# Right sides of half-size products made in 16 steps beside seven plain pairs, and the opening squares on ScalarE

## The chip, the cores and the metric

The kernel runs on one core of a Trainium2 chip. Its time is the device time of one execution in microseconds (us). The kernel before took 2112.32 us (median of three runs, 2112.1 to 2113.64).

A core has five engines, each with its own queue that is worked off in order: TensorE (PE, matmuls; its weight loads are shown as PEld), VectorE (DVE), ScalarE (ACT), GpSimd (POOL) and SyncE (SP, which here issues the DMAs). Matmuls write into PSUM, which has eight banks of 128 x 512 float32.

## The reference, cut to what matters

A decoder trunk of two layers on a sequence of 512 tokens with 1024 channels, all in float32. Each layer has two feed-forwards, so there are four in the kernel; the change touches these alone.

```python
def rms_norm(x, g):
    xf = x.astype(F32)
    y = xf * lax.rsqrt(jnp.mean(xf * xf, axis=-1, keepdims=True) + EPS)
    return (y * g.astype(F32)).astype(x.dtype)

def swiglu_ffn(h, w_in, w_out):          # w_in: 1024 x 5632, w_out: 2816 x 1024
    g, u = jnp.split(h @ w_in, 2, axis=-1)
    return (jax.nn.silu(g) * u) @ w_out
...
    for i in range(DEPTH):               # DEPTH = 2
        x = x + 0.5 * swiglu_ffn(rms_norm(x, ffn1_norm[i]), ffn1_w_in[i], ffn1_w_out[i])
        ...                              # token mixer, cross-attention
        x = x + 0.5 * swiglu_ffn(rms_norm(x, ffn2_norm[i]), ffn2_w_in[i], ffn2_w_out[i])
```

## The kernel before

**Layout and precision.** Activations are held transposed: `x` is eight tiles of 128 channels x 512 tokens. Each float32 operand is split into a high part, a rounded copy made by ScalarE, and a low part, the difference, made by VectorE. A product is three matmuls: high by high, high by low, low by high (`mm3`, lines 395 to 397; the third needs the low part of the weights). The names in the profile: `whl` is a weight tile split in this way (ScalarE's copy at line 326, VectorE's subtraction at line 366), `wraw` the tile as the DMA brought it, `xg` the activations times the norm's gains, split, `hT` the hidden activations, split (lines 407 and 408 are the split of anything but weights).

**The weight stream.** All weights are packed in the order of their use, in tiles of 128 x 512. Four buffers hold raw tiles, seven hold split ones, and the split is issued five tiles ahead of use. A raw tile is fetched when an earlier one's buffer is free.

**A feed-forward** has 22 pairs of output blocks (128 columns of `g` and the 128 of `u`). It runs in this order (`ffn_steps`):

- `first`: pairs 0 and 1 at once, into four banks (`psf`), so that TensorE can start as soon as the first channels are there. On the way `norm_row` forms the norm's factor 1/rms as a row `rbc` spread over all partitions: a matmul with ones (`psn`, line 547), a square root on ScalarE (line 550) and a reciprocal on VectorE (line 551).
- plain pairs up to `NCL`: 48 matmuls of 512 columns each into two banks, `psg` and `psu`. Then `act` multiplies both with `rbc` (lines 601 and 603), takes SiLU on ScalarE (602), and `hidden` multiplies and splits them into `hT` (594, 407, 408).
- the other pairs by seven half-size products each (`seven`): the activations are cut into quarters, and seven sums of weight quarters (the left sides) meet seven sums of activation quarters (the right sides, `rhs`) in 84 matmuls of 256 columns into `psr`. The left sides are sums formed on VectorE (`wsum`, lines 351 to 359). The right sides need the norm applied; `right` forms them once in each feed-forward, for four `j` of 256 channels each: two scalings of `x` (line 616), four subtractions of 256 columns (619 to 622) and the split (407, 408).
- the out-projection (`psy`) in phases: each phase multiplies the hidden blocks that are there (`PHASES`), and `SLOTS` says how many of its eight outputs stand inside each set of seven products.

In the later three feed-forwards `right` is called behind `first`, before any plain pair; in the opening one, where the norm isn't known yet, after the first plain pair. The squares for the norm are made at the end of the stage before, by `squared` (a square on ScalarE, a sum on VectorE); in the opening they are made by GpSimd (line 675) and summed on VectorE (line 677).

**What sets the order.** A scheduler puts the instructions of each engine in a row when the program is built, from the order in which they are written, their dependencies and the free buffers. An engine then takes its row in order; an instruction that waits holds up all behind it. The `tmp` pool has five buffers, for `g`, `u`, squares and the four parts of a `j`.

Of the kernel before, what the change touches and what calls it, by code (L numbers as in the profile page):

```python
# [6 lines left out]
F32 = mybir.dt.float32  # L7
# [6 lines left out]
P = 128  # L14
D = 1024
S = 512
# [3 lines left out]
FK = DFF // P  # L20
# [31 lines left out]
NORMS = (3, 6, 3, 7)  # L52
# [19 lines left out]
def segs_dense(outs, k0=0, k1=DK):  # L72
    for name, c0 in outs:
        for k in range(k0, k1):
            yield (name, k * P, c0, P)


def cols(name, c0, n):
    return [(name, c0 + m * P) for m in range(n)]


def ffn_outs(f, l):
    return [(f"{f}_w_in/{l}", gu * DFF + i * P) for i in range(FK) for gu in range(2)]
# [1 line left out]

PHASES = ((0, 6), (6, 12), (12, 16), (16, FK))
NCL = PHASES[0][1]
SLOTS = (2, 1, 1, 2, 1, 1, 2, 2, 2, 2, 1, 1, 1, 1, 1, 1)  # L90


def ffn_steps():

    yield ("first",)
    for i in range(2, NCL):
        yield ("plain", i)
    outs = iter([("out", p, m) for p in range(len(PHASES) - 1) for m in range(DK)])
    for n in range(NCL, FK):
        for b in (1, 2, 5):  # L100
            yield ("seven", b, n)
        if n > NCL:
            yield ("seven", 4, n - 1)
            yield ("seven", 3, n - 1)
        yield ("seven", 6, n)
        for _ in range(SLOTS[n - NCL]):
            yield next(outs)
        yield ("seven", 7, n)
    yield next(outs)
    yield ("seven", 4, FK - 1)  # L110
    yield ("seven", 3, FK - 1)
    yield from outs
    for m in range(DK):
        yield ("out", len(PHASES) - 1, m)


def segs_ffn(f, l):
    outs, wo = ffn_outs(f, l), cols(f"{f}_w_out/{l}", 0, DK)
    for st in ffn_steps():
# [4 lines left out]
        elif st[0] == "out":  # L124
            if (f, l) == ("ffn2", DEPTH - 1) and st[1:] == (len(PHASES) - 1, DK - 1):
                yield None
            yield from segs_dense([wo[st[2]]], *PHASES[st[1]])
        else:
# [259 lines left out]
class Kernel:  # L388
# [194 lines left out]
    def ffn(self, f, l, gnext, opening=False, mid=(), final=False):  # L583
        nc, ws = self.nc, self.ws
# [4 lines left out]
        with pool(name="ht", bufs=12, reuse_waits="tile") as htp, pool(name="rhs", bufs=DK // 2) as rhsp:  # L589
# [9 lines left out]
            def act(psg, psu):  # L599
                g, u = self.tmp("g"), self.tmp("u")  # L600
                nc.vector.tensor_mul(g, psg, self.rbc)
                nc.scalar.activation(g, g, AF.Silu)
                nc.vector.tensor_mul(u, psu, self.rbc)
                hidden(g, u)

            rhs = []

            def right():


                for j in range(DK // 2):
                    t = rhsp.tile([P, 2, 7, H], F32R, name="rhs")
                    parts = [self.tmp(f"b{i}").rearrange("p (a n) -> p a n", a=2) for i in range(4)]
                    (b11, b12), (b21, b22), (t1, t3), (t2, t4) = ((q[:, 0], q[:, 1]) for q in parts)
                    for h in range(2):
                        nc.vector.scalar_tensor_tensor(parts[h].rearrange("p a n -> p (a n)"), self.x[2 * j + h],
                                                       self.vec(f"{f}_norm/{l}", 2 * j + h), self.rbc,
                                                       op0=ALU.mult, op1=ALU.mult)
                    nc.vector.tensor_sub(t1, b12, b11)
                    nc.vector.tensor_sub(t3, b22, b12)  # L620
                    nc.vector.tensor_sub(t2, b22, t1)
                    nc.vector.tensor_sub(t4, b21, t2)
                    self.split([t[:, p, 0] for p in range(2)], b11)
                    for i in range(3):
                        self.split([t[:, p, 1 + 2 * i:3 + 2 * i] for p in range(2)], parts[1 + i])
                    rhs.append(t)


            SIDES = {1: (0, 0), 2: (1, 1), 3: (2, 2), 4: (6, 0), 5: (3, 2), 6: (5, 0), 7: (4, 0)}
# [31 lines left out]
            outs = ffn_outs(f, l)  # L661
            wo = cols(f"{f}_w_out/{l}", 0, DK)
            last = len(PHASES) - 1
            for st in ffn_steps():
                if st[0] == "first":
                    pss = [self.bank("psf") for _ in range(4)]
                    if opening:
                        for k in range(2):
                            self.gained(k, f"{f}_norm/{l}")
                            ws.split(k + 1)  # L670
                        hooks = {k: lambda k=k: self.gained(k + 2, f"{f}_norm/{l}") for k in range(DK - 2)}
                        self.first(pss, outs[:4], self.xg, hooks=hooks)
                        for k in range(DK):
                            sq = self.tmp("sq") if k else self.bc.tile([P, S], F32, name="sqsum")
                            nc.gpsimd.tensor_mul(sq, self.x[k], self.x[k])
                            if k:
                                nc.vector.tensor_add(self.sqsum, self.sqsum, sq)
                            else:
                                self.sqsum = sq
                    else:  # L680
                        self.first(pss, outs[:4], self.xg, hooks={NORMS[0]: self.norm_row})
                        act(*pss[:2])
                        act(*pss[2:])
                        right()
                elif st[0] == "plain":
                    i = st[1]
                    psg, psu = self.bank("psg"), self.bank("psu")
                    self.dense(psg, outs[2 * i], self.xg)
                    if opening and i == 2:
                        self.norm_row()  # L690
                    self.dense(psu, outs[2 * i + 1], self.xg)
                    if opening and i == 2:
                        act(*pss[:2])
                        act(*pss[2:])
                    act(psg, psu)
                    if opening and i == 2:
                        right()
                elif st[0] == "seven":
                    seven(*st[1:])
                else:  # L700
                    ph, m = st[1:]
                    if final and ph == last:
                        with pool(name="kept", bufs=KEPT) as ws.kept_pool:
                            self.finish(wo, hT, *PHASES[last])
                        return
                    if (ph, m) == (1, 0):
                        next(mid, None)
                    ps = self.bank("psy")
                    self.dense(ps, wo[m], hT, *PHASES[ph])
                    nc.vector.scalar_tensor_tensor(self.x[m], ps, 0.5, self.x[m], op0=ALU.mult, op1=ALU.add)  # L710
                    if ph == last:
                        self.stage_x(m, gnext)
                    elif ph == 1:
                        next(mid, None)
# [825 lines left out]
```

## Time and profile before

| | |
|---|---|
| median of the runs | 2112.32 us |
| profiled execution, its own time | 2111.65 us |
| its span, first to last instruction | 2109.8 us |
| busy: TensorE, VectorE, ScalarE, GpSimd | 98%, 74%, 54%, 9% |
| mean granted TensorE clock | 0.988 of full |
| moved by DMA | 200.91 MB, 95 GB/s in the mean |

Times in the rows are us from the span's start unless marked ns. A row of a timeline gives start, duration, engine, line, instruction, output and inputs, shapes and count, and in brackets how long the engine stood idle before it and what ended that. Durations of one engine's instructions overlap at their ends, so the step from one start to the next is shorter than the duration. The granted clock is given as a share of 2.4 GHz.

### The profile page before, as it was taken

The page shows a single profiled execution, that of the slowest core. Times are in us where ns is not written, and L with a number is a line of the kernel's source. Part 1 is how long each engine was busy: PE and PEld are TensorE (multiplying, and loading weights), DVE is VectorE, ACT ScalarE, POOL GpSimd, SP SyncE. Part 2 cuts the span into 40 slices and gives each one's busy share as a digit, 9 for nine tenths or more (in the row PEclk, how much of TensorE's full clock was granted, in tenths as well). Part 3 has the DMA queues.
Part 4 walks back from the last instruction along what each step waited for, and adds up shares of the span by engine and source line. Part 5 has one row for each costly group of instructions (what it writes and reads, how often), then busy time and mean ns, then how long its engine had stood idle before and what let it go on. Part 6 is the DMA issues. An engine that isn't in the chain of part 4 may idle for free.

```text
span 2109.8 us, 33571 instructions
## 1 busy us (share of the span) xinstructions
PE 2058.1 (98%) x12400; PEld 1836.9 (87%) x12400; DVE 1562.5 (74%) x2834; ACT 1129.9 (54%) x2273; POOL 198.1 (9%) x269
## 2 busy tenths in 40 slices
PE   9799999999989999989999999999999998999997
PEld 6699998988879999878999988788998887899996
DVE  7877876865777777687777767788976557777774
ACT  5455555654535545554545545787775544455453
POOL 2000000000000000000000023444452100000000
PEclk9999999999999999999999999999999999999999
DMA  4333323432233332324332233311124222433222
GB/s 151 100 121 110 105 81 100 146 110 57 74 120 121 101 95 81 98 62 135 120 106 86 73 97 114 98 37 36 66 70 134 76 75 67 133 111 105 91 71 74
DMA packets 112212, 200.91 MB, mean 95 GB/s; under 512 B 12592, under 2 KB 19504, under 8 KB 112048
## 3 DMA queue, kind: packets, MB, share of 16 engines
q1 hardware_dynamic: 111360, 198.20, 30.4%
q8 instruction: 97, 1.59, 0.3%
q10 hardware_dynamic: 688, 0.58, 0.1%
q14 instruction: 67, 0.55, 0.1%
HBM read 196.63 MB, written 2.10 MB: 94 GB/s over the span
## 4 chain that ended last, share of the span: by engine, by line
PE 89%; DVE 7%; ACT 1%; issue 1%; DMA 1%; SPq 0%; DVEq 0%; ACTq 0%
PE psr L397 10%; PE psr L396 10%; PE psr L395 10%; PE psy L396 10%; PE psy L395 10%; PE psy L397 10%; PE pso L1358 2%; PE psq L397 2%; PE psq L396 2%; PE psq L395 2%; DVE rhs L408 2%; PE pst L1346 1%; PE psv L395 1%; PE psv L396 1%; PE psv L397 1%
## 5 line engine op out<-in xcount | busy, mean ns | idle before, releaser
L366 DVE TENSOR_TENSOR whl<-wraw,whl 128x512 fp32r<-128x512 f32 (+2 forms) x631 | 435.4, 693 | 227.4 <-ACT whl L326 213.1
L326 ACT CAST whl<-wraw 128x512 fp32r<-128x512 f32 (+3 forms) x685 | 415.4, 611 | 347.1 <-PE psy L397 92.0
L397 PE MATMUL psr<-rhs,whl 128*128 128x256 f32 x1792 | 506.9, 283 | 1.0 <-DVE whl L366 1.0
L395 PE MATMUL psr<-rhs,whl 128*128 128x256 f32 x1792 | 507.5, 283 | 0.2
L396 PE MATMUL psr<-rhs,whl 128*128 128x256 f32 x1792 | 507.1, 283 | 0.0
L395 PEld LDWEIGHTS psr<-rhs,whl 128*128 128x128 f32 x1792 | 343.5, 192 | 4.3 <-ACT whl L326 1.4
L396 PEld LDWEIGHTS psr<-rhs,whl 128*128 128x128 f32 x1792 | 343.5, 192 | 2.8
L397 PEld LDWEIGHTS psr<-rhs,whl 128*128 128x128 f32 x1792 | 343.2, 192 | 2.0 <-DVE whl L366 1.8
L396 PE MATMUL psy<-hT,whl 128*128 128x512 f32 (+1 forms) x710 | 276.2, 389 | 0.0
L395 PE MATMUL psy<-hT,whl 128*128 128x512 f32 (+1 forms) x710 | 275.9, 389 | 0.0
L397 PE MATMUL psy<-hT,whl 128*128 128x512 f32 (+1 forms) x710 | 275.1, 388 | 0.0
L326 ACT CAST whl<-wsum 128x512 fp32r<-128x512 f32 x256 | 159.3, 622 | 203.7 <-PE psy L397 155.6
L366 DVE TENSOR_TENSOR whl<-wsum,whl 128x512 fp32r<-128x512 f32 x256 | 176.1, 689 | 56.1 <-ACT whl L326 53.9
L397 PEld LDWEIGHTS psy<-hT,whl 128*128 128x128 f32 x710 | 133.4, 188 | 27.6
L396 PEld LDWEIGHTS psy<-hT,whl 128*128 128x128 f32 x710 | 133.6, 188 | 25.7 <-DVE hT L408 1.2
L395 PEld LDWEIGHTS psy<-hT,whl 128*128 128x128 f32 x710 | 133.6, 188 | 25.4
L366 POOL TENSOR_TENSOR whl<-wraw,whl 128x512 fp32r<-128x512 f32 (+2 forms) x54 | 70.0, 1298 | 846.2 <-ACT whl L326 840.8
L710 DVE SCALAR_TENSOR_TENSOR x<-psy,x 128x512 f32<-128x512 f32 x120 | 82.6, 689 | 43.3 <-PE psy L397 42.5
L1339 POOL TENSOR_SCALAR pr<-pr,smn,gates 128x128 f32<-128x128 f32 (+3 forms) x128 | 87.7, 696 | 98.7 <-DVE smn L1337 70.0
L397 PE MATMUL psu<-xg,whl 128*128 128x512 f32 x128 | 54.0, 422 | 29.1 <-DVE whl L366 29.1
L1330 ACT ACTIVATE pr<-pr,mxn 128x128 f32<-128x128 f32 (+3 forms) x128 | 71.3, 559 | 17.0 <-DVE mxn L1326 15.8
L395 PE MATMUL psq<-xg,whl 128*128 128x512 f32 x192 | 75.8, 395 | 0.0
(308 smaller groups left out, 3957.1 us busy)
## 6 DMA issues: line engine op xcount, KB each, us to landing
wraw<-wts SPq DMA_DIRECT2D x711, 256.0 KB, 2.8
wraw<-wts SPq DMA_DIRECT2D x18, 128.0 KB, 2.5
wraw<-wts SPq DMA_DIRECT2D x12, 192.0 KB, 2.5
x<-xT SPq DMA_DIRECT2D x8, 256.0 KB, 5.3
mraw<-memT SPq DMA_DIRECT2D x4, 512.0 KB, 3.6
out<-y SPq DMA_DIRECT2D x6, 256.0 KB, 2.6
wraw<-wts SPq DMA_DIRECT2D x8, 152.0 KB, 2.2
out<-y ACTq DMA_DIRECT2D x2, 256.0 KB, 2.9
```

Of the source, the lines that this page charges most:

```text
L326: nc.scalar.copy(self.hl[q][:, 0, :w], src[:, :w])
L366: eng.tensor_sub(hl[:, 1, :w], src[:, :w], hl[:, 0, :w].bitcast(F32))
L395: mm(ps, a[0], b[0], start=start, stop=False, **kw)
L396: mm(ps, a[0], b[1], start=False, stop=False, **kw)
L397: mm(ps, a[1], b[0], start=False, stop=stop, **kw)
L408: self.nc.vector.tensor_sub(hl[1], src, hl[0].bitcast(F32))
L710: nc.vector.scalar_tensor_tensor(self.x[m], ps, 0.5, self.x[m], op0=ALU.mult, op1=ALU.add)
L1330: nc.scalar.activation(pr[br][:, :nk], pr[br][:, :nk], AF.Exp, bias=mx[:, br:br + 1], scale=-1.0, accum_out=sums[:, br:br + 1])
L1339: nc.gpsimd.tensor_scalar(pr[br][:, :nk], pr[br][:, :nk], sums[:, br:br + 1], gt[:, i, h * 3 + 1 + br:h * 3 + 2 + br], op0=ALU.mult, op1=A ...
L1346: nc.tensor.transpose(pt[:, j * P:(j + 1) * P], pr[br][:, j * P:(j + 1) * P], self.identf)
L1358: nc.tensor.matmul(ps[:, c0:c0 + 256], v[br][j][:, g, :], pT[br][:, hl, j, :], start=False, stop=br == 1 and j == 2 * i2 + 1 and hl == 1)
```

## The change

The seven-product stage starts one pair later (`PHASES` begins with 7 in place of 6, and the second phase of the out-projection has 5 blocks in place of 6; `SLOTS` is fitted to it). `right` becomes a generator `rights` with four stops for each `j`, 16 in all. In the later three feed-forwards its first two steps are taken inside `first`, at channels 6 and 7; the rest are taken in the plain pairs, one for every five of the matmul groups that `dense_steps` counts, seven to a bank. What isn't done by the end of the last plain pair follows behind it. In the opening the steps begin in the second bank of the first plain pair, so that 12 of them stand beside pairs. The opening squares are made by `squared`, on ScalarE.

```diff
-PHASES = ((0, 6), (6, 12), (12, 16), (16, FK))
+PHASES = ((0, 7), (7, 12), (12, 16), (16, FK))
 NCL = PHASES[0][1]
-SLOTS = (2, 1, 1, 2, 1, 1, 2, 2, 2, 2, 1, 1, 1, 1, 1, 1)
+SLOTS = (2, 2, 2, 1, 1, 2, 2, 2, 2, 1, 1, 1, 1, 1, 1)
...
-            def right():
+            def rights():
...
                                                        op0=ALU.mult, op1=ALU.mult)
+                    yield
                     nc.vector.tensor_sub(t1, b12, b11)
                     nc.vector.tensor_sub(t3, b22, b12)
                     nc.vector.tensor_sub(t2, b22, t1)
                     nc.vector.tensor_sub(t4, b21, t2)
+                    yield
                     self.split([t[:, p, 0] for p in range(2)], b11)
                     for i in range(3):
                         self.split([t[:, p, 1 + 2 * i:3 + 2 * i] for p in range(2)], parts[1 + i])
+                        if i != 1:
+                            yield
                     rhs.append(t)
+
+            right = rights()
+
+            def plain(ps, out):
+
+                nonlocal count
+                for _ in self.dense_steps(ps, out, self.xg):
+                    count += 1
+                    if count % 5 == 0:
+                        next(right, None)
+
+            count = 0
...
                         for k in range(DK):
-                            sq = self.tmp("sq") if k else self.bc.tile([P, S], F32, name="sqsum")
-                            nc.gpsimd.tensor_mul(sq, self.x[k], self.x[k])
-                            if k:
-                                nc.vector.tensor_add(self.sqsum, self.sqsum, sq)
-                            else:
-                                self.sqsum = sq
+                            self.squared(k)
                     else:
-                        self.first(pss, outs[:4], self.xg, hooks={NORMS[0]: self.norm_row})
+                        self.first(pss, outs[:4], self.xg, hooks={NORMS[0]: self.norm_row, 6: lambda: next(right),
+                                                                 7: lambda: next(right)})
                         act(*pss[:2])
                         act(*pss[2:])
-                        right()
                 elif st[0] == "plain":
                     i = st[1]
                     psg, psu = self.bank("psg"), self.bank("psu")
-                    self.dense(psg, outs[2 * i], self.xg)
                     if opening and i == 2:
+                        self.dense(psg, outs[2 * i], self.xg)
                         self.norm_row()
-                    self.dense(psu, outs[2 * i + 1], self.xg)
+                    else:
+                        plain(psg, outs[2 * i])
+                    plain(psu, outs[2 * i + 1])
...
-                    if opening and i == 2:
-                        right()
+                    if i == NCL - 1:
+                        for _ in right:
+                            pass
```

Lines of the changed kernel behind the generator stand some 14 to 16 further down; `right`'s subtractions are lines 620 to 623 there.

**VectorE, second feed-forward (ffn2 of layer 0).** Before, the end of the block of right sides (`b` are the parts of a `j`) and the first low halves of weights (`whl`) behind it:

```order
L408 TENSOR_TENSOR rhs<-b_5775,rhs 128x256
L622 TENSOR_TENSOR b_5778<-b_5776,b_5778 128x256
L408 TENSOR_TENSOR rhs<-b_5776,rhs 128x512
L408 TENSOR_TENSOR rhs<-b_5777,rhs 128x512
L408 TENSOR_TENSOR rhs<-b_5778,rhs 128x512
L366 TENSOR_TENSOR whl<-wraw,whl 128x512 x2
L601 TENSOR_TENSOR g<-psg,rbc 128x512
```

Now, in the second plain pair of the same feed-forward:

```order
L366 TENSOR_TENSOR whl<-wraw,whl 128x512
L623 TENSOR_TENSOR b_5784<-b_5782,b_5784 128x256
L408 TENSOR_TENSOR rhs<-b_5781,rhs 128x256
L408 TENSOR_TENSOR rhs<-b_5782,rhs 128x512
L366 TENSOR_TENSOR whl<-wraw,whl 128x512
L601 TENSOR_TENSOR g<-psg,rbc 128x512
L366 TENSOR_TENSOR whl<-wraw,whl 128x512
L408 TENSOR_TENSOR rhs<-b_5783,rhs 128x512
L408 TENSOR_TENSOR rhs<-b_5784,rhs 128x512
L366 TENSOR_TENSOR whl<-wraw,whl 128x512
```

The low halves of weights now stand between the steps of a `j`, where before all four `j` stood in one piece with none among them.

**VectorE, opening feed-forward, behind the last plain pair.** Before, from the sum for the third product to the low halves behind the last read of `psu`:

```order
L353 TENSOR_TENSOR wsum<-wsum,wraw_661 128x512
L366 TENSOR_TENSOR whl<-wraw_664,whl 128x512
L366 TENSOR_TENSOR whl<-wsum,whl 128x512 x2
L603 TENSOR_TENSOR u<-psu,rbc 128x512
L366 TENSOR_TENSOR whl<-wraw,whl 128x512
L594 TENSOR_TENSOR u<-u,g 128x512
```

Now, from that read on:

```order
L603 TENSOR_TENSOR u<-psu,rbc 128x512
L616 SCALAR_TENSOR_TENSOR b_827<-x_109,vecsb,rbc 128x512
L594 TENSOR_TENSOR u<-u,g 128x512
L616 SCALAR_TENSOR_TENSOR b_828<-x_110,vecsb,rbc 128x512
L620 TENSOR_TENSOR b_829<-b_827 128x256
L408 TENSOR_TENSOR hT<-u,hT 128x512
L621 TENSOR_TENSOR b_829<-b_828,b_827 128x256
L622 TENSOR_TENSOR b_830<-b_828,b_829 128x256
L408 TENSOR_TENSOR rhs<-b_827,rhs 128x256
L623 TENSOR_TENSOR b_830<-b_828,b_830 128x256
L408 TENSOR_TENSOR rhs<-b_828,rhs 128x512
L408 TENSOR_TENSOR rhs<-b_829,rhs 128x512
```

The fourth `j` (of `x` 6 and 7) now stands here, behind the read of the last pair's second bank. Ahead of that read stand the same rows as before.

**TensorE at the same place**, now, with buffer numbers (`rhs_826` is the right side of the fourth `j`, the three `psr` belong to the first three products):

```order
L397 MATMUL psr_885<-rhs_698,whl_759 128x256
L395 MATMUL psy_927<-hT_438,whl_800 128x512
L396 MATMUL psy_927<-hT_438,whl_800 128x512
L395 MATMUL psy_956<-hT_438,whl_846 128x512
L396 MATMUL psy_956<-hT_438,whl_846 128x512
L395 MATMUL psr_845<-rhs_826,whl_708 128x256
L395 MATMUL psr_866<-rhs_826,whl_740 128x256
L395 MATMUL psr_885<-rhs_826,whl_759 128x256
L396 MATMUL psr_845<-rhs_826,whl_708 128x256
L397 MATMUL psr_845<-rhs_826,whl_708 128x256
```

Before, the first product ran through all four `j` before the second began; now the first three products take their first three `j`, and four out-projection matmuls are drawn forward, before the fourth.

## Rows read from the trace of the kernel before

**Rows 1.** Page, parts 1 and 4: busy share of TensorE; last chain by engine
```profile
PE 2058.1 (98%) x12400; PEld 1836.9 (87%) x12400; DVE 1562.5 (74%) x2834; ACT 1129.9 (54%) x2273; POOL 198.1 (9%) x269
...
PE 89%; DVE 7%; ACT 1%; issue 1%; DMA 1%; SPq 0%; DVEq 0%; ACTq 0%
```

**Rows 2.** Waits of TensorE over the whole span: us in total, times, longest
```profile
PE psu L397 <- DVE whl L366: 29.1, 4, 10.6
PE psf L397 <- DVE whl L366: 2.8, 2, 2.3
```

**Rows 3.** Timeline of VectorE, second feed-forward: start, us, instruction, idle before and its releaser
```profile
561.80 0.69 DVE L366 TENSOR_TENSOR whl<-wraw,whl 128x512 fp32r<-128x512 f32 x1 [2.03 <-ACT whl L326]
...
572.02 1.41 DVE L616 SCALAR_TENSOR_TENSOR b<-x,vecsb,rbc 128x512 f32<-128x512 f32 x2
573.34 0.42 DVE L619 TENSOR_TENSOR b<-b 128x256 f32<-128x256 f32 x1
573.68 0.42 DVE L620 TENSOR_TENSOR b<-b,b 128x256 f32<-128x256 f32 x1
...
576.83 1.41 DVE L616 SCALAR_TENSOR_TENSOR b<-x,vecsb,rbc 128x512 f32<-128x512 f32 x2
...
586.44 1.29 DVE L366 TENSOR_TENSOR whl<-wraw,whl 128x512 fp32r<-128x512 f32 x2
587.65 0.69 DVE L601 TENSOR_TENSOR g<-psg,rbc 128x512 f32<-128x512 f32 x1
```

**Rows 4.** Timeline of TensorE, second feed-forward, where it starts again
```profile
587.19 0.79 PE L397 MATMUL psu<-xg,whl 128*128 128x512 f32 x1 [6.18 <-DVE whl L366]
...
593.24 0.39 PE L397 MATMUL psu<-xg,whl 128*128 128x512 f32 x1
...
599.82 0.39 PE L395 MATMUL psu<-xg,whl 128*128 128x512 f32 x1
```

**Rows 5.** Timeline of TensorE, the same feed-forward, first half-size product
```profile
616.13 0.28 PE L395 MATMUL psr<-rhs,whl 128*128 128x256 f32 x1
...
617.45 0.28 PE L397 MATMUL psr<-rhs,whl 128*128 128x256 f32 x1
```

**Rows 6.** Busy by stretch: us, PE, PEld, DVE, ACT, POOL (x), clock, DMA, GB/s
```profile
70.40:73.90 3.50, 3.40 (x8) 2.73 (x9) 3.50 (x7) 1.59 (x3) 0.00 (x0) 0.51 0.41 152
587.10:592.70 5.60, 5.51 (x13) 4.35 (x14) 5.60 (x11) 2.29 (x4) 0.00 (x0) 0.51 0.51 165
944.60:947.60 3.00, 2.96 (x7) 2.38 (x8) 3.00 (x6) 1.14 (x2) 0.00 (x0) 0.50 0.45 166
1784.50:1790.60 6.10, 6.00 (x14) 4.75 (x15) 4.46 (x9) 2.09 (x4) 0.00 (x0) 0.50 0.58 175
17.00:22.00 5.00, 2.69 (x12) 1.91 (x11) 5.00 (x8) 0.62 (x1) 1.48 (x1) 1.00 0.12 15
625.00:700.00 75.00, 75.00 (x521) 70.31 (x521) 60.62 (x102) 37.00 (x73) 0.00 (x0) 1.00 0.39 122
```

**Rows 7.** Timeline of GpSimd, opening
```profile
7.81 5.58 POOL L675 TENSOR_TENSOR sq<-x 128x512 f32<-128x512 f32 x4 [0.87 <-DMA x<-xT]
```

**Rows 8.** Timeline of VectorE, opening and start of its half-size products
```profile
10.96 1.52 DVE L366 TENSOR_TENSOR whl<-wraw,whl 128x512 fp32r<-128x512 f32 x1
...
86.14 0.69 DVE L366 TENSOR_TENSOR whl<-wraw,whl 128x512 fp32r<-128x512 f32 x1 [3.09 <-ACT whl L326]
...
91.40 0.69 DVE L603 TENSOR_TENSOR u<-psu,rbc 128x512 f32<-128x512 f32 x1
```

**Rows 9.** Timeline of ScalarE, opening
```profile
4.46 0.72 ACT L492 ACTIVATE xg<-x,vecsb 128x512 fp32r<-128x512 f32 x1 [1.74 <-DMA x<-xT]
```

**Rows 10.** Timeline of TensorE, opening, start of its half-size products
```profile
87.60 0.28 PE L395 MATMUL psr<-rhs,whl 128*128 128x256 f32 x1
...
94.28 0.40 PE L395 MATMUL psy<-hT,whl 128*128 128x512 f32 x1
```

**Rows 11.** Timeline of ScalarE, a square of the later stages
```profile
542.93 0.62 ACT L505 ACTIVATE sq<-x 128x512 f32<-128x512 f32 x1
```

## The prediction

> **What bounds the kernel now.** I read the page first: TensorE is busy for 98% of the span, and the chain that ended last runs through it for 89% and through VectorE for 7% [rows 1]. So VectorE holds TensorE up somewhere, and the next view, TensorE's waits, says where: 29.1 us in four waits, the longest 10.6, all `psu` matmuls waiting for the low half of a weight tile (`whl`, line 366) [rows 2]. There are four feed-forwards, and each has one such wait.
>
> The third view is VectorE's timeline at one of them, the second (ffn2 of layer 0) [rows 3]. The low half at 561.80 is the last for a long time. Then VectorE multiplies out the heads of the first four banks and after that makes all right sides in one block: one `j` begins at 572.02, the next at 576.83, so a `j` takes 4.81 us and the four 19.2. The next low half stands at 586.44, 24.6 us after the last. TensorE starts again at 587.19 after 6.18 us of waiting [rows 4], so it ran dry at 581.0. It had lived on tiles split ahead for 18.6 us from the end of the last low half (about 562.4). Those 18.6 us are the lead with which I reckon below.
>
> Fourth, the stretches with their granted clock [rows 6]: after each of the four waits TensorE goes on at a clock of 0.50 to 0.51, which is the 1.2 GHz level. At 2.4 GHz a 512-wide matmul takes 0.227 us (29 steps from 593.24 to 599.82 [rows 4]) and a 256-wide one 0.120 (11 steps from 616.13 to 617.45 [rows 5]). In the stage of the half-size products TensorE is busy for 75.00 us of 75.00 and VectorE for 60.62 [rows 6]: nothing but the number of matmuls counts there.
>
> **The change, part by part.** I reckon against the profiled execution: span 2109.8, its own time 2111.65; the median of the runs is 2112.32, 0.67 more.
>
> (a) The block of right sides leaves VectorE's queue in front of the low halves. Its instructions stay the same: per `j` two scalings, four 256-wide subtractions, one 256-wide and three 512-wide low halves. Only their place changes: 14 of the 16 steps stand beside the plain pairs, two inside the first four banks. By the order of the second feed-forward there is now never more than about 4.5 us of other work between two low halves of plain tiles (four low halves of right sides, one of them 256 wide, and four reads of `psf`: 0.34 + 7 x 0.60 [rows 3]; 0.60 is half of 586.44 to 587.65, 0.34 is 573.34 to 573.68). Does VectorE's total fit? A plain pair takes TensorE 48 x 0.227 = 10.9 us. It costs VectorE four low halves and four instructions of `act`, 8 x 0.60 = 4.8, and now 19.2 / 5 = 3.84 of right sides: 8.6 of 10.9 us. With 18.6 us of lead at the start and less work than time, TensorE should not run dry in the last three feed-forwards, and the first wait of the opening goes as well. Gone: 29.1 us, and 4 x 0.16 = 0.6, since a wait is counted from a modelled end 0.39 after the matmul's start where the next would have started after 0.23. Bounds: none of it gone if the low halves were late again (rival 3), 29.7 at most.
>
> (b) With the waits go the falls of the clock. The four stretches at half clock are 3.50, 5.60, 3.00 and 6.10 us with 8, 13, 7 and 14 matmuls [rows 6]; at 0.227 each these would take 1.8, 3.0, 1.6 and 3.2. That is 8.6 us lost to the clock.
>
> (c) A seventh plain pair replaces one set of seven products in each feed-forward. Seven products are 84 matmuls of 256 columns, 84 x 0.120 = 10.1 us; a pair is 48 of 512, 10.9. TensorE is the bound in both, so 0.8 us, times four: +3.3. The out-projections keep their matmuls: 7 + 5 steps in place of 6 + 6. The Trainium skill (TensorE: Matmul & The Clock Gate, section "Back-to-back issue gap") gives a gap of N/2.4 + 2.5 ns, 216 and 109 ns; by it the difference would be 1.2 us a set, 4.7 in all, and the sum 1.4 higher. The rows show 227 and 120, and a row decides.
>
> (d) The opening squares go from GpSimd to ScalarE. GpSimd makes four of them in 5.58 us [rows 7], and while it does, VectorE's 512-wide low half takes 1.52 us [rows 8] where it takes 0.60 to 0.69 elsewhere [rows 3]. That slowness is why the fifth tile's low half is late and TensorE waits 2.3 us, its longest on `psf` [rows 2, 6]. After the change ScalarE's queue up to the fifth cast holds eight scaled copies, five squares and four casts; at no more than 0.72, 0.62 and 0.6 [rows 3, 9, 11] they run from 4.46 to about 15.7 us. The low half then stands at about 16.9, and TensorE wants it at 18.1 (17.0 plus five steps). So the wait goes, 2.31 + 0.16. In return the first square stands ahead of the first cast, and TensorE starts 0.6 later. Net -1.9; bounds -2.5 (that square hidden) and +0.6 (the wait comes back elsewhere).
>
> (e) The tail of the first feed-forward is new. There `norm_row` comes late, only 12 steps fit beside the pairs, and by the order the whole fourth `j` stands behind the last read of `psu`. In the kernel before that read stood at 91.40, TensorE having begun its products at 87.60 [rows 8, 10]: 3.8 us after the pairs' end, because the sums and low halves for the first products stand in front of it. The same rows stand in front of it now. Counted from the pairs' end: the read to 4.4; scaling, `u*g`, scaling (0.66, 0.60, 0.66) to 6.3; subtraction, `hT`, two subtractions (0.34, 0.60, 0.34, 0.34) to 7.9; low half of 256, subtraction, low half of 512 (0.34, 0.34, 0.60) to 9.2; the next low half, which the third product needs, ends at 9.9. TensorE has by then done what it can without the fourth `j`, and 11 matmuls are left: 11.2. In the kernel before it was there after 94.28 - 87.60 = 6.7 [rows 10], and four 512-wide matmuls (0.9) are now done earlier: 11.2 - 6.7 - 0.9 = +3.6. Bounds: 0 if other work fills it, 6.3 if nothing is done in between.
>
> (f) The clock in that tail. The waits there, broken by a few matmuls, come to some 4.5 us. A wait of 2.3 us left the clock at 1.00; waits of 6.2 and more brought 0.5 [rows 2, 6]. 4.5 lies nearer to 6.2, so I take a fall at the mean price of the four, 8.6 / 4 = +2.2; bounds 0 and 2.9. The Trainium skill (the same page, section "HAM oscillation — how this bites in real kernels") says that waits between groups of matmuls throttle the array anew. By that rule the fall comes, and the sum stays as below; by the row of 2.3 us it would be 2.2 lower. No wait of 4.5 us is in this trace.
>
> Sum: 2111.65 - 29.7 - 8.6 + 3.3 - 1.9 + 3.6 + 2.2 = 2080.6, and with 0.67 for the median 2081.2.
>
> **The rivals.**
> 1. No tail. TensorE finds enough to do in the first feed-forward: without (e) and (f) 2075.4. For it: four out-projection matmuls are already drawn forward. Against: the products need the fourth `j`, and its 12 rows stand in one piece behind the read.
> 2. A tail in all four feed-forwards: three times 3.6 + 2.2 more, 2098.6. For it: VectorE has 8.6 of 10.9 us filled, and it stops twice per pair for a bank. Against: there the last right side stands in front of the read of `psg`, some 5 us before the pairs' end.
> 3. The change doesn't do what it says: low halves come late inside the pairs in one or two of the four feed-forwards, so that about a third of (a) and (b), 12.8 us, comes back: 2094. For it: ScalarE's casts of right sides now stand between casts of weight tiles that wait for a buffer. Against: the lead of 18.6 us.
> 4. Slower. The lead is gone, and the first low half after each read of `psu` is always late. In front of it stand a scaling, `u*g`, a scaling, three subtractions and `hT`, 0.66 + 0.60 + 0.66 + 3 x 0.34 + 0.60 = 3.5 us, and its own 0.6: 4.1 us, plus a fall of the clock at 2.2. In the four later pairs of each feed-forward, 16 times, that is 101 us against the waits saved: 2181. It decides from the point where the lead is under 4.1 us; five such pairs (31 us) eat up the gain.
>
> **How the numbers follow.** The forecast has a chance of 0.70, with a range of its own of 2076 to 2087 (the bounds of d, e and f). Rival 1 has 0.10, rival 2 0.08, rival 3 0.08, rival 4 0.04. 2073 to 2094 leaves out rivals 2 and 4 and half of 3. Faster or slower by 0.2% is about 4 us, what a measurement of this kernel tells from no change. Only rival 4, and a part of rival 3 in which everything returns, are not faster by that much: faster 0.94, same 0.03, slower 0.03.
>
> **What would show it.** (a) No wait of `psu` matmuls for line 366 over 1 us, and low halves spread among the right sides. (b) A clock of 1.00 in the plain pairs of the last three feed-forwards. (c) 144 matmuls fewer, and an unchanged step. (d) No squares on GpSimd, low halves under 0.7 us and no wait of 2.3 us at the opening. (e) and (f) A wait of `psr` matmuls for right sides of 3 to 5 us, once, near 85 us, and a clock of 0.5 behind it. I'm wrong if waits for `whl` stay, if `psr` waits in each feed-forward, or if the time is above 2094.

## The result, and the profile after

The changed kernel takes 2079.64 us (median of four runs, 2076.10 to 2080.61) against 2112.98 of the kernel before (2112.10 to 2114.11): a ratio of 0.9839, 95% interval 0.9822 to 0.9856. The profiled execution is the longest of the four, 2080.61 us with a span of 2078.9.

Parts 1 and 4 of the page after, busy time by engine and the last chain, which answer to [rows 1]:

```profile
PE 2056.1 (99%) x12256; PEld 1829.8 (88%) x12256; DVE 1537.7 (74%) x2810; ACT 1123.0 (54%) x2261; POOL 184.6 (9%) x261
...
PE 93%; DVE 4%; DMA 1%; ACT 1%; issue 1%; POOL 0%; SPq 0%; DVEq 0%; ACTq 0%; POOLq 0%
```

There are 144 matmuls fewer, as forecast, and TensorE's share of the chain grew from 89 to 93%. The waits of TensorE, in place of [rows 2]: total us, times, longest.

```profile
PE psr L395 <- ACT rhs L407: 2.0, 2, 1.1
...
PE psf L395 <- ACT whl L326: 1.4, 1, 1.4
...
PE psr L397 <- DVE whl L366: 1.0, 4, 0.3
```

The `psu` line of 29.1 us is gone and so is the 2.3 us of `psf`. In the opening a low half takes 0.68 us, against 1.52 in [rows 8]:

```profile
11.25 0.68 DVE L366 TENSOR_TENSOR whl<-wraw,whl 128x512 fp32r<-128x512 f32 x1
```

VectorE's timeline at the same feed-forward as [rows 3]:

```profile
552.83 2.22 DVE L408 TENSOR_TENSOR rhs<-b,rhs 128x256 fp32r<-128x256 f32 x4
...
557.37 0.68 DVE L366 TENSOR_TENSOR whl<-wraw,whl 128x512 fp32r<-128x512 f32 x1
...
565.33 0.69 DVE L366 TENSOR_TENSOR whl<-wraw,whl 128x512 fp32r<-128x512 f32 x1 [2.03 <-ACT whl L326]
567.39 0.69 DVE L603 TENSOR_TENSOR u<-psu,rbc 128x512 f32<-128x512 f32 x1 [1.37 <-PE psu L397]
...
571.53 0.69 DVE L366 TENSOR_TENSOR whl<-wraw,whl 128x512 fp32r<-128x512 f32 x1
572.14 0.42 DVE L623 TENSOR_TENSOR b<-b,b 128x256 f32<-128x256 f32 x1
572.47 1.02 DVE L408 TENSOR_TENSOR rhs<-b,rhs 128x256 fp32r<-128x256 f32 x2
573.41 0.69 DVE L366 TENSOR_TENSOR whl<-wraw,whl 128x512 fp32r<-128x512 f32 x1
```

A low half (`whl`) now stands between the pieces of every `j` of this feed-forward. The piece reckoned at 4.5 us (four low halves of right sides and four reads of `psf`) runs from 552.83 to 557.37, 4.5 us; the next longest between low halves of plain tiles, from 567.39 to 571.53, takes 4.1. Before, 24.6 us lay between two low halves. The plain pairs of the last three feed-forwards by stretch, columns as in [rows 6]:

```profile
556.40:610.70 54.30, 54.30 (x241) 44.96 (x240) 38.86 (x69) 22.61 (x40) 0.00 (x0) 1.00 0.31 90
...
905.60:959.90 54.30, 54.30 (x241) 44.98 (x240) 38.89 (x69) 22.64 (x40) 0.00 (x0) 1.00 0.30 91
1738.80:1793.10 54.30, 54.30 (x242) 44.95 (x240) 38.85 (x69) 22.59 (x39) 0.00 (x0) 1.00 0.30 91
```

TensorE is busy all the time at the full clock. The table gives TensorE's stages from the first matmul's start to the last one's end, in us, read off both timelines; the opening's plain pairs are taken from behind the norm's matmuls, without their first bank.

| stage | before | after | difference |
|---|---|---|---|
| opening, up to the end of the first banks | 31.34 | 29.95 | -1.4 |
| plain pairs, opening | 50.69 | 49.15 | |
| plain pairs, the other three | 52.68, 51.50, 53.01 | 54.56, 54.56, 54.56 | +4.95 with the line above |
| products and out-projections, opening | 282.96 | 278.58 | -4.4 |
| the same, the other three | 282.86, 282.63, 282.65 | 272.75, 272.97, 272.55 | -29.9 |
| all else | | | -0.3 |

The four added pairs are 4 x 48 x 0.2273 = 43.65 us of matmuls, so the pairs lost 43.65 - 4.95 = 38.7 us of waits and half clock.

### The profile page after: what moved, and what is told of

Same layout as the page of the kernel before. It is cut to its first block, busy times and chain, and to the rows that moved or that the text cites. A ratio compares the mean times of both kernels' runs of the same rounds, so it can differ in the third digit from the quotient of the medians.

```text
span 2078.9 us, 33307 instructions
## 1 busy us (share of the span) xinstructions
PE 2056.1 (99%) x12256; PEld 1829.8 (88%) x12256; DVE 1537.7 (74%) x2810; ACT 1123.0 (54%) x2261; POOL 184.6 (9%) x261
## 4 chain that ended last, share of the span: by engine, by line
PE 93%; DVE 4%; DMA 1%; ACT 1%; issue 1%; POOL 0%; SPq 0%; DVEq 0%; ACTq 0%; POOLq 0%
PE psy L396 10%; PE psy L395 10%; PE psy L397 10%; PE psr L397 10%; PE psr L396 10%; PE psr L395 10%; PE pso L1372 2%; PE psq L397 2%; PE psq L395 2%; PE psg L396 2%; PE psg L395 2%; PE psg L397 2%; PE psq L396 2%; PE psu L397 2%; PE psu L396 2%; PE psu L395 2%
## 5 line engine op out<-in xcount | busy, mean ns | idle before, releaser
L326 ACT CAST whl<-wraw 128x512 fp32r<-128x512 f32 (+2 forms) x697 | 419.8, 606 | 381.6 <-PE psy L397 112.9
L395 PE MATMUL psr<-rhs,whl 128*128 128x256 f32 x1680 | 476.7, 284 | 2.4 <-ACT rhs L407 2.0
L397 PE MATMUL psr<-rhs,whl 128*128 128x256 f32 x1680 | 475.8, 284 | 1.1 <-DVE whl L366 1.0
L396 PE MATMUL psr<-rhs,whl 128*128 128x256 f32 x1680 | 476.0, 283 | 0.3 <-DVE rhs L408 0.3
L395 PEld LDWEIGHTS psr<-rhs,whl 128*128 128x128 f32 x1680 | 322.4, 192 | 7.4 <-ACT rhs L407 2.8
L396 PEld LDWEIGHTS psr<-rhs,whl 128*128 128x128 f32 x1680 | 322.4, 192 | 3.2 <-DVE rhs L408 0.5
L397 PEld LDWEIGHTS psr<-rhs,whl 128*128 128x128 f32 x1680 | 322.3, 192 | 2.3 <-DVE whl L366 2.1
L326 ACT CAST whl<-wsum 128x512 fp32r<-128x512 f32 x240 | 149.4, 622 | 172.0 <-PE psy L397 136.2
L366 DVE TENSOR_TENSOR whl<-wsum,whl 128x512 fp32r<-128x512 f32 x240 | 165.1, 689 | 77.1 <-ACT whl L326 77.0
L395 PE MATMUL psq<-xg,whl 128*128 128x512 f32 x192 | 76.0, 396 | 0.0
L396 PE MATMUL psq<-xg,whl 128*128 128x512 f32 x192 | 75.6, 394 | 0.0
```

Source lines behind the costliest of these rows:

```text
L326: nc.scalar.copy(self.hl[q][:, 0, :w], src[:, :w])
L366: eng.tensor_sub(hl[:, 1, :w], src[:, :w], hl[:, 0, :w].bitcast(F32))
L395: mm(ps, a[0], b[0], start=start, stop=False, **kw)
L396: mm(ps, a[0], b[1], start=False, stop=False, **kw)
L397: mm(ps, a[1], b[0], start=False, stop=stop, **kw)
```

## The experiments

**The spreading alone: `e2_block`.** Seven pairs and ScalarE's squares stay; only the right sides go back into a block.

```diff
-                    count += 1
-                    if count % 5 == 0:
-                        next(right, None)
+                    pass
...
-self.first(..., hooks={NORMS[0]: self.norm_row, 6: lambda: next(right), 7: lambda: next(right)})
+self.first(..., hooks={NORMS[0]: self.norm_row})
 act(*pss[:2])
 act(*pss[2:])
+for _ in right:
+    pass
...
-if i == NCL - 1:
+if opening and i == 2:
     for _ in right:
         pass
```

> The changed kernel with seven plain pairs and the squares on ScalarE, but the right sides made in one block where the kernel before had it (behind the first banks, in the opening behind the first plain pair). Theory (the spreading alone removes the waits): waits of psu for line 366 of about 29 us in four come back, with 8.6 us of half clock, and the opening's tail of 5.8 us goes: 2079.6 + 29.7 + 8.6 - 5.7 = 2112; the plain stages of the last three feed-forwards are 54.6 + 7 to 9 us. Rival (the seventh pair or the squares removed them): under 2090.

Measured: 2114.86 us, ratio to before 1.0012 (1.0003 to 1.0021). Its waits of TensorE:

```profile
PE psu L397 <- DVE whl L366: 29.0, 4, 10.5
```

The same four waits as in [rows 2]; the pairs take 62.63, 63.66, 63.39 and 62.50 us, 39.4 more than in the changed kernel, and the opening's products 5.4 less. The theory stands: without the spreading the rest of the change brings nothing (it costs 2.5 us).

**The lead: `e6_before_six` and `e7_after_five`.**

```diff
-    RAW, HL, AHEAD = 4, 7, 5
+    RAW, HL, AHEAD = 4, 6, 4      (kernel before)
+    RAW, HL, AHEAD = 4, 5, 3      (changed kernel)
```

> The kernel before with six buffers for split weight tiles in place of seven, and the split four tiles ahead. Theory (TensorE outlives the block of right sides only by the tiles split ahead, 18.6 us, and a tile is 12 matmuls, 12 x 0.2275 = 2.73 us): each of the four psu waits for line 366 grows by 2.7 us, 29.1 becomes 40.0, and the time about 2112.3 + 10.9 = 2123, apart from what other stages lose. Rival (the wait is set by something else than the number of split tiles, as the raw tiles' DMA): the four waits stay at 29 us.

Measured: 2123.92 us, ratio 1.0053 (1.0038 to 1.0068); the waits:

```profile
PE psg L397 <- DVE whl L366: 38.0, 4, 12.8
```

The waits grow by 8.9 us, 2.2 each where I had said 2.7, and come one output earlier (`psg`). The pairs are longer by 3.0, 1.7, 2.7 and 2.2. The direction is the theory's, the size is four fifths of it. The trace shows why: in the second feed-forward TensorE gets through 76 matmuls of the pairs before it runs dry in the kernel before and through 66 here, ten fewer and not twelve (10 x 0.227 = 2.3). A tile less is twelve less, but behind the last low half that it has, TensorE's row holds six matmuls that need none here, and four in the kernel before.

> The changed kernel with five buffers for split weight tiles, split three tiles ahead. Theory (there is never more than about 4.5 us of other work between two low halves): the lead falls from 18.6 to 18.6 - 2 x 2.73 = 13.1 us, still far above 4.5, so the plain stages stay at 49.15 and 54.56 us and the four feed-forwards lose nothing there; what the other stages lose is not forecast. Rival (the spread right sides live on the lead too, as in the fourth rival of the prediction): waits for whl come behind the reads of psu, and the plain stages of the last three grow by over 2 us each.

Measured: 2085.05 us; the pairs take 49.15, 54.56, 54.56 and 54.56, to the hundredth what they took with seven buffers. The 5.4 us are lost elsewhere (of the 4.7 us between the profiled executions, 2.1 lie in the opening's products and 1.5 in the later ones). With two tiles less of lead nothing comes late beside the pairs: the prediction's third and fourth rivals fall.

**The pair for a set: `e1_six_pairs`.**

```diff
-PHASES = ((0, 7), (7, 12), (12, 16), (16, FK))
+PHASES = ((0, 6), (6, 12), (12, 16), (16, FK))
...
-                    if count % 5 == 0:
+                    if count % 4 == 0:
```

> The changed kernel with six plain pairs as before, and a step of the right sides after every fourth group of three matmuls in place of every fifth; the 16 steps then fit beside the pairs of the last three feed-forwards as they did, and in the opening 12 fit, as they did. Theory (TensorE is the bound and only its matmuls count): a set of seven products is 0.8 us shorter than a plain pair, four times, so 3.3 us less than the changed kernel, about 2076.4; the plain stage of the last three feed-forwards is 192 x 0.2275 = 43.7 us. Rival (VectorE becomes the bound): a pair now costs it 4.8 + 19.2 / 4 = 9.6 of 10.9 us, waits for whl come back and the time is no better than the changed kernel's 2079.6.

Measured: 2075.78 us (2075.12 to 2077.16). In the second feed-forward pairs and products take 43.68 + 282.89 = 326.57 where they took 54.56 + 272.75 = 327.31: 0.74 for one pair against one set. In the mean of the last three feed-forwards it is 0.70 against the changed kernel (327.32 with seven pairs) and 0.95 against `e4_no_tail` (327.57), so the price is known to a quarter of a us. VectorE keeps up; the seventh pair wasn't needed for the spreading, it costs.

**The tail: `e4_no_tail` and `e5_tail_all`.** The first takes steps faster in the opening, the second lets every feed-forward end with four steps open.

```diff
-                    if count % 5 == 0:
+                    if count % (4 if opening else 5) == 0:
                         next(right, None)
+                if opening:
+                    count += 1
+                    if count % 4 == 0:
+                        next(right, None)
```
```diff
-                    if count % 5 == 0:
+                    if count % 5 == 0 and count <= (60 if opening else 50):
```

> The changed kernel with a step after every fourth group in the opening feed-forward (counted over the gaps between two outputs too), so that all 16 steps stand beside its pairs. Theory (the opening's products wait for the fourth j of the right sides): the waits of psr for right sides near 85 to 95 us and the half clock behind them go, and the first stage of products is shorter by 5.7 us, what it measures above its matmuls: 2074. Rival (the left sides, with their sums and their tiles by DMA, hold the products up there as well): a part of it stays as psr or psy waits for whl, and the gain is under 3 us. Second rival: VectorE is too full at that rate and waits for whl appear in the opening's pairs.

Measured: 2075.96 us (2074.69 to 2077.29). For the tail, first the changed kernel's TensorE at the opening's first products (idle time in brackets):

```profile
84.68 0.28 PE L395 MATMUL psr<-rhs,whl 128*128 128x256 f32 x1
...
90.18 0.40 PE L396 MATMUL psy<-hT,whl 128*128 128x512 f32 x1
...
92.08 0.38 PE L395 MATMUL psr<-rhs,whl 128*128 128x256 f32 x1 [1.10 <-ACT rhs L407]
93.35 0.38 PE L395 MATMUL psr<-rhs,whl 128*128 128x256 f32 x1 [0.89 <-ACT rhs L407]
...
94.65 0.37 PE L395 MATMUL psr<-rhs,whl 128*128 128x256 f32 x1
...
97.45 0.63 PE L397 MATMUL psy<-hT,whl 128*128 128x512 f32 x1
97.88 0.63 PE L395 MATMUL psy<-hT,whl 128*128 128x512 f32 x1
```

and VectorE's row for which all this waits, and TensorE's stretch at half clock behind it:

```profile
88.77 0.68 DVE L603 TENSOR_TENSOR u<-psu,rbc 128x512 f32<-128x512 f32 x1
```
```profile
94.90:98.30 3.40, 3.40 (x16) 3.21 (x16) 3.40 (x7) 1.80 (x4) 0.00 (x0) 0.53 0.27 93
```

In `e4_no_tail` TensorE goes from the first product to the first out-projection in 6.97 us without a wait over 0.28:

```profile
83.13 0.28 PE L395 MATMUL psr<-rhs,whl 128*128 128x256 f32 x1
...
86.16 0.39 PE L397 MATMUL psr<-rhs,whl 128*128 128x256 f32 x1 [0.28 <-DVE whl L366]
...
90.10 0.40 PE L395 MATMUL psy<-hT,whl 128*128 128x512 f32 x1
```

The first stretch of products, up to the next `psn`, falls from 121.45 to 116.04 us: the tail cost 5.4. The medians differ by 3.7 and the profiled executions by 5.9 (this one began at the full clock, see below), so the price is taken from the stretch.

> The changed kernel with at most 12 steps of the right sides taken up to the end of the plain pairs in each of the four feed-forwards (two of them inside the first banks in the last three), so that the fourth j stands behind the last read of psu everywhere, as it does in the opening. Theory (that place is what makes the tail): each of the last three feed-forwards grows by what the opening lost to it, 121.45 - 116.04 = 5.4 us: 2079.6 + 16.2 = 2095.8, with psr waits for right sides in each and a piece of half clock behind them. Rival (the opening's tail comes from its late norm, and elsewhere TensorE finds other matmuls): under 2 us each, under 2086.

Measured: 2097.18 us (2097.05 to 2099.92), 17.5 more. The waits:

```profile
PE psr L395 <- ACT rhs L407: 7.9, 8, 1.1
```

Eight waits where there were two; products of the last three are 5.9, 5.5 and 5.1 longer, and the granted clock falls to 0.50 behind each of the four tails. The place of the last `j` makes the tail, not the opening's late norm.

**The squares: `e8_squares_late` and `e3_pool_squares`.** The first begins the sum at the third channel tile. The token mixer of this kernel leaves out the fresh start of one sum of squares, which runs on from an older sum: one addition more, outside the feed-forwards, and an output that is not the reference's. The later kernels with this edit start that sum afresh. The second puts the squares back on GpSimd, as in the removed lines of the change.

```diff
-        if k == 0:
+        if start:
...
-for k in range(DK):
-    self.squared(k)
+for k in (2, 3, 4, 5, 6, 7, 0, 1):
+    self.squared(k, start=k == 2)
```

> The changed kernel with the sum of squares begun at the third channel tile, so that the squares of the first two come last, and no square stands ahead of the first two casts of weight tiles. Theory (the first square delays the first cast, TensorE's first wait grows from 0.90 to 1.40 us, and its first seven matmuls run at half clock): TensorE starts 0.5 us earlier at the full clock, 7 x 0.2 = 1.4 us more, 1.9 in all: 2077.7, and the first banks end near 28.0 instead of 29.95. Rival (what is late at the opening is a tile or a low half): it waits as much a few matmuls further on, and the gain is under 0.5 us.

Measured: 2079.41 us (2078.81 to 2080.24), the same as the changed kernel. TensorE starts 0.43 us earlier (5.81), but its first matmuls run at half clock all the same and the first banks end at 29.39, 0.56 earlier. My theory for the half clock falls: the wait was 0.96 us here, and in `e4_no_tail` 1.66 with the full clock:

```profile
6.24 0.80 PE L395 MATMUL psf<-xg,whl 128*128 128x512 f32 x1 [1.40 <-ACT whl L326]
6.83 0.63 PE L396 MATMUL psf<-xg,whl 128*128 128x512 f32 x1
7.26 0.63 PE L395 MATMUL psf<-xg,whl 128*128 128x512 f32 x1
```
```profile
6.33 0.50 PE L395 MATMUL psf<-xg,whl 128*128 128x512 f32 x1 [1.66 <-ACT whl L326]
6.66 0.40 PE L396 MATMUL psf<-xg,whl 128*128 128x512 f32 x1
6.90 0.40 PE L395 MATMUL psf<-xg,whl 128*128 128x512 f32 x1
```

The first piece is the changed kernel's (steps of 0.43), the second that of `e4_no_tail` (0.24), whose opening is written like the changed kernel's up to there.

> The changed kernel with the opening's squares back on GpSimd. Theory (GpSimd's squares slow VectorE's low halves from 0.68 to 1.52 us, and that makes the opening's wait of 2.3 us): that wait and the low halves of 1.5 us return, TensorE starts 0.5 us earlier, and the first banks end at 31.3 where they end at 28.4 with the full clock and 29.9 with the half clock at the start: 1.4 to 2.9 us more than the changed kernel, 2081.0 to 2082.5. Rival (the first seven matmuls' half clock comes from the later start with ScalarE's squares): 4 of 5 profiles with ScalarE's squares at full and half clock would be no chance, and this one starts at the full clock as the kernel before did.

Measured: 2083.22 us (2081.03 to 2084.18), 3.6 more than the changed kernel. Its TensorE:

```profile
5.92 0.79 PE L395 MATMUL psf<-xg,whl 128*128 128x512 f32 x1 [1.07 <-ACT whl L326]
6.51 0.65 PE L396 MATMUL psf<-xg,whl 128*128 128x512 f32 x1
...
20.97 0.50 PE L397 MATMUL psf<-xg,whl 128*128 128x512 f32 x1 [1.65 <-DVE whl L366]
```

and VectorE's low half beside GpSimd's squares:

```profile
12.02 1.52 DVE L366 TENSOR_TENSOR whl<-wraw,whl 128x512 fp32r<-128x512 f32 x1
```

The wait is back, low halves take 1.52 us again, and the first banks end at 31.70, 1.75 later than in the changed kernel. The rest is not the squares': of the 3.0 us between the profiled executions, the opening's products give back 1.3, and 2.6 come in later stages that the edit doesn't touch. The half clock comes with GpSimd's squares too, so the rival falls as well.

**A better version: `e9_six_no_tail`, then three with tables of their own.** `e9_six_no_tail` takes back the three things that had cost: the pair, the tail, the first square.

> Six plain pairs, no tail, and the opening's squares begun at the third channel tile, at once: a step after every fourth group in the last three feed-forwards, after every third in the opening. Theory (the three add up, since each takes matmuls or waits from TensorE, which is the bound): 0.74 x 4 = 3.0 less for the pairs, 5.4 for the tail, 0.5 for the squares: 2079.6 - 8.9 = 2070.7. Rival (VectorE is full at a step in every third group, 4.8 + 6.4 = 11.2 of 10.9 us a pair): waits for whl in the opening's pairs take back 2 us or more, 2073 or above.

Measured: 2075.33 us (2074.68 to 2077.85), not 2070.7. TensorE's stretches in the opening's pairs and first products, columns as in [rows 6], and two waits there:

```profile
38.00:73.00 35.00, 35.00 (x156) 29.00 (x155) 34.55 (x59) 19.04 (x32) 0.00 (x0) 1.00 0.25 76
73.60:78.00 4.40, 2.84 (x21) 2.43 (x20) 4.40 (x11) 2.86 (x5) 0.00 (x0) 1.00 0.13 50
78.00:84.40 6.40, 5.55 (x24) 4.97 (x23) 6.40 (x12) 3.58 (x7) 0.00 (x0) 0.50 0.07 22
```
```profile
76.96 0.39 PE L397 MATMUL psr<-rhs,whl 128*128 128x256 f32 x1 [1.07 <-DVE whl L366]
80.30 0.58 PE L397 MATMUL psr<-rhs,whl 128*128 128x256 f32 x1 [0.85 <-DVE whl L366]
```

VectorE (34.55 of 35.00 us) enters the products without a break, their left sides come late, and the clock falls: the rival's way, though behind the pairs and not in them. So the opening keeps its seven pairs, as in `e4_no_tail`, and the other three get a table of their own, here that with four pairs:

```diff
+TABLE = {True: (((0, 7), (7, 12), (12, 16), (16, FK)), ...),
+         False: (((0, 4), (4, 12), (12, 16), (16, FK)), (1, 1, 1, 1, 1, 1, 1, 1, 2, 2, 2, 2, 1, 1, 1, 1, 1, 1))}
...
-                    if count % 5 == 0:
+                    if count % (4 if opening else 2) == 0:
```

> Seven plain pairs with a step every fourth group in the opening feed-forward (no tail), six plain pairs in the other three, also with a step every fourth group; the opening's squares begun at the third tile. Theory (what was lost when six pairs met the missing tail was VectorE in the opening alone): 2076.0 - 3 x 0.74 - 0.5 = 2073.2, with no wait over 1 us in the four feed-forwards. Rival (a set of seven instead of a pair gains nothing by itself, because VectorE forms its left sides): 2075.5 or above.

> The same with five plain pairs in the last three feed-forwards and a step after every third group there. Theory (the lead of 18.6 us covers a VectorE that has 4.8 + 6.4 = 11.2 us of work for a pair's 10.9 us): three sets less by 0.74 again, 2071.0. Rival (from here VectorE is the bound: low halves, or the left sides of the first products, come late): waits for whl of 2 us or more in each of the three, the time at or above that of six pairs.

> The same with four plain pairs in the last three feed-forwards and a step after every second group. VectorE then has 4.8 + 9.6 = 14.4 us of work for a pair's 10.9 us, 7 us too much in two pairs. Theory (the lead of 18.6 us covers that): 2068.8. Rival (VectorE enters the products late by these 7 us and its left sides come late, as in the opening with six pairs and no tail): 4 us or more lost in each of the three, the time above that of six pairs.

Measured: 2072.78 (2071.26 to 2073.50), 2070.67 (2068.05 to 2072.36) and 2069.81 us (2068.10 to 2071.34); the last is 0.9794 of before (0.9780 to 0.9807). The forecast sums hold to 1 us, but the ranges overlap: the medians alone don't part five pairs from four. Pairs and products of the second to fourth feed-forward, in the mean: 327.6 with seven pairs (`e4_no_tail`), 326.6, 325.8 and 325.3. The last step gives 0.5 where the first two gave 0.9 and 0.8. In its pairs VectorE has no room left, and behind them, in each of the three feed-forwards, stands a wait for ScalarE's copy of a bank, which the kernels with five and six pairs don't have (lines stand two further down here):

```profile
551.50:573.20 21.70, 21.70 (x98) 17.96 (x97) 21.43 (x42) 11.13 (x20) 0.00 (x0) 1.00 0.29 89
```
```profile
PE psr L397 <- ACT g L674: 1.4, 3, 0.5
```

ScalarE makes that copy at 580.10 us, behind the cast of a sum for which it waited on VectorE. That VectorE's full pairs cause the wait is likely by this order and was not tried by itself.

## Why the prediction was right

2081.2 was worked out for the median and 2080.6 for the profiled execution; 2079.64 and 2080.61 were measured. The mechanism came as forecast; the agreement of the profiled execution to 0.1 us is luck, since errors cancel, and the median lay 1.0 below it where I had added 0.67. By its terms:

- **(a) and (b), waits and half clock**: -38.3 forecast, -38.7 measured in the table; `e2_block` brings them back (39.4), and `e7_after_five` shows that the lead had room.
- **(c) the seventh pair**: 0.8 each forecast, 0.74 by `e1_six_pairs` (0.70 to 0.95 in the mean of three). The Trainium skill's gap (TensorE: Matmul & The Clock Gate, section "Back-to-back issue gap") would give 1.2, an estimate from its formula; the trace disagrees, with 0.227 us for each 512-wide matmul of a pair (54.56 / 240).
- **(d) the squares**: -1.9 forecast. The end of the first banks moved by -1.4 in the profiled execution, which began at half clock, and by -2.9 in `e2_block` (28.36) and `e4_no_tail` (28.41), which didn't. Against `e3_pool_squares` (31.70), also half clock at first, it is -1.75. The mechanism is right; that the start's clock enters the term wasn't seen.
- **(e) the tail**: +3.6 forecast. `e3_pool_squares` has the same tail without a fall of the clock, and its first stretch of products is 120.12 - 116.04 = 4.1. The read of `psu` ended 4.8 us behind the pairs (88.77 + 0.68 - 84.68), forecast 4.4.
- **(f) the clock in the tail**: +2.2 forecast, 5.4 - 4.1 = 1.3 measured, in a shorter stretch (3.4 us at 0.53) than the mean of [rows 6]. The waits came to 3.4 us and not 4.5 (90.18 to 94.65, less one matmul at 0.23 and seven at 0.12), in pieces of which the longest are 1.1 and 0.9: my sign for (e) and (f), one wait of 3 to 5 us, was wrong in form.

That the clock can fall at such short waits was to be read from the kernel before. Between its third and fourth feed-forward it fell to 0.50 within the second of two waits of 1.46 and 1.83 us, with a few matmuls between them; [rows 6] leaves this stretch out:

```profile
1321.65 0.33 PE L395 MATMUL psk<-hidT,whl 128*128 128x128 f32 x1 [1.46 <-ACT hidT L407]
...
1324.45 0.48 PE L396 MATMUL psk<-hidT,whl 128*128 128x128 f32 x1 [1.83 <-DVE hidT L408]
```
```profile
1323.20:1329.80 6.60, 5.35 (x20) 4.87 (x21) 4.22 (x10) 2.67 (x8) 1.20 (x2) 0.50 0.27 85
```

So the reading that 2.3 us left the clock at 1.00 and 6.2 and more brought 0.5 was too simple: the length of a single wait doesn't decide. Of the nine tails in the traces (the changed kernel, `e1_six_pairs`, `e3_pool_squares`, four in `e5_tail_all`, `e7_after_five`, `e8_squares_late`) eight have a piece at 0.50. That of `e3_pool_squares` has none, with the same waits (1.09 and 0.89 us) as the changed kernel: a fall there is likely, not certain, and what decides it stays open. The Trainium skill (same page, section "HAM oscillation — how this bites in real kernels") tells of groups of matmuls that start anew at the low clock after each wait, in its case after longer waits than these; eight tails of nine agree.

The errors of (d), +0.5, (e), +0.5, and (f), -0.9, cancel. Rivals 1 and 2, priced at 2075.4 and 2098.6, were made in `e4_no_tail` and `e5_tail_all` and took 2075.96 and 2097.18.

## What to carry to other kernels

Where an engine that feeds the bound engine also does other work, compare its longest block of that work with the bound engine's stock, both in us. If the block is longer, cut it into steps between the feeding instructions, and see to it that the last step is done before the stage that needs it. Then ask what was put in only to make room (here the seventh pair), and take it back stage by stage, until the feeding engine's busy time fills the stretch (21.43 of 21.70 us here). Stop earlier where the next stage needs that engine at once: in `e9_six_no_tail` 34.55 of 35.00 us was too much.

## What was not expected of the hardware

TensorE begins at half clock in some executions and not in others, also where the opening is the same: of the five kernels that share the changed kernel's opening and its buffers, `e2_block` and `e4_no_tail` had no slow matmul there, and the changed kernel, `e1_six_pairs` and `e5_tail_all` had seven or eight. Of the 14 profiled executions, three (the kernel before, `e2_block`, `e4_no_tail`) ran all their first matmuls at the full clock, 11 had a piece at steps of 0.43 us in the first five microseconds of matmuls. The Trainium skill (TensorE: Matmul & The Clock Gate, section "What's actually happening") says that the number of slow matmuls at a start varies from run to run; the traces agree, with none in three executions and seven to eleven in the others. It costs 1.65 us where nothing hides it (first banks 23.71 against 22.05 to 22.08) and 0.2 where a later wait does (25.78 in `e3_pool_squares`, 25.59 before). The view of stretches shows 1.00 there, since the recorded clock begins later (at 9.75 us in the changed kernel's trace); only the step of the matmuls tells:

```profile
6.20:9.20 3.00, 2.96 (x7) 2.39 (x8) 2.98 (x5) 3.00 (x6) 0.00 (x0) 1.00 1.01 376
```

These are seven matmuls in 3.0 us at a clock given as 1.00. Some of the changed kernel's spread of 4.5 us between runs may come from this and from (f); that was not tried.
